# The end of a streaming encoder layer: the sample's stores on GpSimd's queue, the root as TensorE's diagonal, and the first piece of the last token block in halves

## The chip, the cores and the metric

The kernel runs on one core of one Trainium2 chip. The metric is the device time of one execution in microseconds (us). Three timed runs of the kernel before gave a median of 1300.93 us, the lowest 1300.31 and the highest 1302.64.

## The reference

One layer (DEPTH is 1) of a hybrid encoder runs on two request groups that share their weights: 256 new prompt positions (`x_prompt`) and 32 positions of a running stream (`x_sample`). Cut to what matters here:

```
D_MODEL = 2048;  SEQ = 256;  DEC_SEQ = 32;  D_FF = 5632;  EPS = 1e-6

def rmsnorm(x, g):
    y = xf * lax.rsqrt(jnp.mean(xf * xf, axis=-1, keepdims=True) + EPS)
    return (y * g).astype(x.dtype)

def run_layer(x, ...):
    xn = rmsnorm(x, norm_mix_pre);  proj = xn @ w_in
    y_pool = pool_mixer(...);  y_ssd = ssd_mixer(...)
    mix = concat[y_pool, y_ssd] @ w_out
    x = x + rmsnorm(mix, norm_mix_post)
    hn = rmsnorm(x, norm_ffn_pre)
    up = causal_dwconv(hn @ w_up, ...)
    f = (silu(gate) * val) @ w_down
    x = x + rmsnorm(f, norm_ffn_post)      # the part that the change touches
    return x, ...
```

The outputs are the two new `x` (`y_prompt` and `y_sample`, 32-bit floats) and the states of the pooling, the convolutions and the state-space mixer. The change touches only the last line: every row of `f` (one row per token, 2048 columns) has its sum of squares, the root of the mean, its reciprocal (the factor), the weights `norm_ffn_post`, and the residual `x`.

## The kernel before, in words

Everything up to the last product is held with features on the 128 partitions and the 288 tokens (256 of the prompt, 32 of the sample) along the free axis, 16 blocks of 128 features. The three large stages (`w_in`, `w_up`, `w_down`, and `w_out` between) stream their weights from memory through SP's queue in pieces of up to 1 MB; ScalarE and VectorE split each piece into a high and a low part (lines 153 and 154), and TensorE multiplies three times per block (line 167).

The end begins with the last two feature blocks of the down projection, A and B (lines 1300 to 1379). By then the other 14 blocks have been multiplied by their weights, turned through DRAM (`fd`) and loaded back with tokens on the partitions: `ft[2*q+b]` holds quarter `q` (512 columns) of token block `b` (128 tokens: `b` = 0 the first, `b` = 1 the last half of the prompt), `ft_s` the 32 sample tokens with their four quarters on four groups of 32 partitions. `xr[2*q+b]` and `xr_s` hold the residual in the same form, loaded long before.

For the last token block (`b` = 1) and the sample, A and B are computed first, their sums of squares go through TensorE (`other_sums`, line 1267), and `rf` (line 1276 the root on ScalarE, line 1277 the reciprocal on VectorE) is their factor. TensorE then goes on with the first token block (`b` = 0), whose 256 columns it computes with tokens on the partitions at once (`p_0`, line 1365). While it does, VectorE finishes the others: `y_out(q, b, rf)` writes `ft * rf + xr` into `xr` with one scalar_tensor_tensor of 128x512 (line 1385) and stores it on SP's queue (line 1386). The order before is quarters 0, 1 and 2 of `b` = 1, then the sample (line 1390, four stores at line 1392), then quarter 3.

When `p_0` is done, ScalarE squares it with a sum (line 1399), VectorE weighs it with `g_row` into `ft[6]` (line 1400), ScalarE takes the root and VectorE the reciprocal (lines 1276 and 1277 again, the factor of `b` = 0). Quarter 0 of `b` = 0 is TensorE's: `p_y` gets identity times `xr[0]` (line 1403) and, once ScalarE has scaled the identity by the factor (`diag`, line 1406), diag times `ft[0]` (line 1407). ScalarE copies `p_y` to SBUF (line 1408) and issues its store on its own queue (line 1411). Quarters 1, 2 and 3 of `b` = 0 are VectorE's, with `y_out`.

All of this is written between `pin(...)`, which keeps an engine's pinned instructions in the order of the program; SP's queue issues in that order too, and a store that waits holds up those behind it. Each token block has four quarters of 256 KB, the sample 256 KB in four stores of 64 KB.

Of the kernel before, what the change touches and what calls it, by code (L numbers as in the profile page):

```python
# [8 lines left out]
F32 = mybir.dt.float32  # L9
F32R = mybir.dt.float32r  # L10
AF = mybir.ActivationFunctionType
ALU = mybir.AluOpType
# [3 lines left out]
P = 128  # L16
TC = {"schedule_with_timeline_sim": True}
D_MODEL = 2048
# [52 lines left out]
def body(  # L71
# [23 lines left out]
    act, dve, pool, pe, sp = nc.scalar, nc.vector, nc.gpsimd, nc.tensor, nc.sync  # L95
# [36 lines left out]
    pin = tc.keep_in_program_order  # L132
# [90 lines left out]
    start = ExitStack()  # L223
# [41 lines left out]
    for name, n in COLS:  # L265
        c0 = sum(m.shape[1] for m in col.values())
# [9 lines left out]
    ident = const.tile([P, P], F32, name="ident")  # L276
# [3 lines left out]
        out=tri, in_=ones, pattern=[[1, P]], compare_op=ALU.is_ge, fill=0.0, base=0, channel_multiplier=-1  # L280
# [79 lines left out]
    for i, (kb, n) in enumerate(CHUNKS):  # L360
# [26 lines left out]
        for q, (r, m, k, x) in enumerate(products):  # L387
            if i == len(CHUNKS) - 1 and q == 0:
# [10 lines left out]
                start=kb + k + r + x == 0, stop=kb + k == KD - 1 and r == 1,  # L399
            ))  # L400

    for k in range(KD):
        c = slice(HEADS * (k % 4), HEADS * (k % 4 + 1))
# [7 lines left out]
    c0 = 3 * NXC + 3 * KD  # L411
# [82 lines left out]
    with tc.high_priority(offset=EVAC):  # L494
        for i, v in enumerate(v4):
            c = slice(HEADS * i, HEADS * (i + 1))
# [488 lines left out]
    for gi in range(2):  # L985
        c = slice(gi * P, (gi + 1) * P)
# [168 lines left out]
    fp = ffn.enter_context(tc.tile_pool(name="ffn", bufs=1))  # L1155
# [83 lines left out]
    xr = []  # L1239
# [8 lines left out]
    ft = [apool.tile([P, 512], F32, tag="a", name="ft") for _ in range(6)]  # L1248
# [25 lines left out]
    def factors(src, bias, n, name):  # L1274
        o = side1.tile([P, 2], F32, tag="trs", bufs=2, name=name)[:, :n]
        pin(act.activation(o, src, AF.Sqrt, bias=bias, scale=1.0 / D_MODEL))
        pin(dve.reciprocal(o, o))
        return o
# [40 lines left out]
    g_row = late_[:, 4 * P :]  # L1319
# [4 lines left out]
    p_0 = acc_ps.tile([P, 2 * P], F32, tag="acc", name="acc_t")  # L1324
# [12 lines left out]
    for n_, part_ in enumerate(parts):  # L1337
        for i, t in enumerate((A, B)):
            for k, hi, lo in part_:
                c, end = slice(i * P, (i + 1) * P), k == HALF - 1  # L1340
# [8 lines left out]
    bias_0 = fp.tile([P, 1], F32, name="bias_0")  # L1349
# [13 lines left out]
    for k, hi, lo in sum(parts, []):  # L1363
# [4 lines left out]
        if k == SUMS_AT:  # L1368
            other_sums(sq[0])
            rf = factors(p_f, eps_t, 2, "rf1")  # L1370
# [7 lines left out]
                    p_0[:, i * P : (i + 1) * P], part[t][:, C0], ident, start=False, stop=False, skip_group_check=True  # L1378
                ))

    def y_out(q, b, rf):

        x = xr[2 * q + b]
        f_ = last if (q, b) == (3, 1) else ft[2 * q + b]
        pin(dve.scalar_tensor_tensor(x, f_, rf, x, op0=ALU.mult, op1=ALU.add))  # L1385
        pin(sp.dma_start(out=y_prompt[0][b * P : (b + 1) * P, 512 * q : 512 * (q + 1)], in_=x))

    for q in range(3):
        y_out(q, 1, rf[:, 0:1])
    pin(dve.scalar_tensor_tensor(xr_s, ft_s, rf[:, 1:2], xr_s, op0=ALU.mult, op1=ALU.add))  # L1390
    for q in range(4):
        pin(sp.dma_start(
            out=y_sample[0][:, 512 * q : 512 * (q + 1)], in_=xr_s[NS * q : NS * (q + 1), :]
        ))
    y_out(3, 1, rf[:, 0:1])

    sum_0 = fp.tile([P, 1], F32, name="sum_0")
    sq_0 = fp.tile([P, 290], F32, tag="fc", bufs=6, name="sq_0")
    pin(act.activation(sq_0[:, : 2 * P], p_0, AF.Square, accum_out=sum_0))
    pin(dve.tensor_tensor(ft[6][:, 2 * P :], p_0, g_row, op=ALU.mult))  # L1400

    p_y = acc_ps.tile([P, 512], F32, tag="acc", name="py_")
    pin(pe.matmul(p_y, ident, xr[0], start=True, stop=False))
    rf = factors(sum_0, bias_0, 1, "rf0")
    diag = fp.tile([P, P], F32, tag="fc", bufs=6, name="diag")
    pin(act.activation(diag, ident, AF.Copy, scale=rf[:, 0:1]))
    pin(pe.matmul(p_y, diag, ft[0], start=False, stop=True))
    pin(act.activation(xr[0], p_y, AF.Copy))
    y_out(1, 0, rf[:, 0:1])
    y_out(2, 0, rf[:, 0:1])  # L1410
    pin(act.dma_start(out=y_prompt[0][0:P, 0:512], in_=xr[0]))
    y_out(3, 0, rf[:, 0:1])
    ffn.close()


# [65 lines left out]
```

## Time and profile before

| what | value |
|---|---|
| timed runs, median (lowest to highest) | 1300.93 us (1300.31 to 1302.64) |
| the profiled execution's own time | 1302.5 us |
| its span, first to last instruction | 1300.8 us |
| TensorE busy | 1292.3 us, 99% of the span |
| VectorE busy | 900.2 us, 69% |
| ScalarE busy | 670.9 us, 52% |
| GpSimd busy | 255.0 us, 20% |
| bytes over the DMA queues | 251.81 MB, mean 194 GB/s |
| granted TensorE clock | 1.000 |

Times in the trace count from the span's start. An instruction's row has its start, its duration, engine, line and operands; a row with "x3" merges three in a row. The "q" behind an engine (SPq, ACTq) marks its queue issuing a transfer: such a row says how long the issue took, not when the bytes arrived. That is in the groups of DMA issues, as microseconds from issue to landing. The view by windows gives the busy time of each engine and what the DMA engines moved in each stretch. The end that the change touches is the stretch from 1290 us on.

### The profile page before, as it was taken

The numbers are of one execution on the slowest core, as the hardware profiler recorded it, in microseconds if no ns is written. First come the engines' busy times: TensorE is split into PE (matmuls) and PEld (weight loads), VectorE is DVE, ScalarE is ACT, GpSimd is POOL, SyncE is SP. The second block draws the span as 40 slices with busy tenths as digits, with TensorE's granted clock in tenths as the row PEclk, the third lists the DMA queues.
The fourth block names the chain that finished last, engine by engine and source line by source line (L and its number), as shares of the span: only waits on it lengthen the run. The fifth ranks groups of instructions, "written<-read, shape, count | busy, mean of one in ns | idle before, by whom it ended". The sixth has DMA issues, their size and how long they took to land.

```text
span 1300.8 us, 25801 instructions
## 1 busy us (share of the span) xinstructions
PE 1292.3 (99%) x10283; PEld 1284.9 (99%) x10283; DVE 900.2 (69%) x1546; ACT 670.9 (52%) x1013; POOL 255.0 (20%) x407
## 2 busy tenths in 40 slices
PE   9999999999999999999999999999999999999998
PEld 9999999999999999999999999999999999999997
DVE  7899998998655688877766744336666666755454
ACT  7554976656544466544444443334444454444442
POOL 3433332122232231211211200001111121201110
PEclk9999999999999999999999999999999999999999
DMA  9578887355766478766545444555545555466763
GB/s 353 172 214 245 272 258 241 131 183 162 257 206 225 143 198 256 209 177 200 176 162 175 165 161 173 166 170 185 168 162 167 176 173 167 162 232 189 215 180 116
DMA packets 110648, 251.81 MB, mean 194 GB/s; under 512 B 65088, under 2 KB 74208, under 8 KB 88256
## 3 DMA queue, kind: packets, MB, share of 16 engines
q1 hardware_dynamic: 104144, 233.52, 55.9%
q0 software_dynamic: 5952, 16.13, 4.4%
q8 instruction: 80, 1.31, 0.4%
q10 hardware_dynamic: 432, 0.52, 0.1%
q14 instruction: 40, 0.33, 0.1%
HBM read 237.13 MB, written 13.00 MB: 192 GB/s over the span
## 4 chain that ended last, share of the span: by engine, by line
PE 95%; issue 2%; DMA 1%; ACT 1%; POOL 0%; DVE 0%; SPq 0%; POOLq 0%; ACTq 0%
PE acc L167 89%; PE acc L397 1%; DMA raw<-in_w_first 1%; PE acc_x L167 1%; PE acc_x L397 1%; PE acc L1342 1%; PE acc L1343 0%; DMA mg<-in_x_g 0%; PE py L678 0%; PE py_l L678 0%; PE acc_t L1365 0%; ACT w L330 0%; POOL ho L1073 0%; PE acc L404 0%; DVE xr L1385 0%
## 5 line engine op out<-in xcount | busy, mean ns | idle before, releaser
L154 DVE TENSOR_TENSOR wlo<-raw,whi 128x1024 fp32r<-128x1024 f32 (+1 forms) x396 | 472.7, 1196 | 285.6 <-ACT whi L153 284.7
L153 ACT ACTIVATE whi<-raw 128x1024 fp32r<-128x1024 f32 (+1 forms) x396 | 407.7, 1032 | 445.4 <-PE acc L167 362.6
L167 PE MATMUL acc<-hn,whi 128*128 128x288 f32 x2752 | 539.1, 294 | 0.7 <-ACT hn L1118 0.4
L167 PEld LDWEIGHTS acc<-hn,whi 128*128 128x128 f32 x2752 | 436.5, 188 | 1.8 <-ACT hn L1118 0.9
L167 PE MATMUL acc<-hn,wlo 128*128 128x288 f32 x1376 | 399.7, 291 | 0.0
L167 PEld LDWEIGHTS acc<-hn,wlo 128*128 128x128 f32 x1376 | 258.9, 188 | 0.0
L167 PE MATMUL acc<-fa,whi 128*128 128x288 f32 x1320 | 257.5, 293 | 0.0
L167 PE MATMUL acc<-xn,whi 128*128 128x288 f32 x1216 | 238.6, 294 | 0.0
L167 PEld LDWEIGHTS acc<-fa,whi 128*128 128x128 f32 x1320 | 208.9, 188 | 0.0
L167 PEld LDWEIGHTS acc<-xn,whi 128*128 128x128 f32 x1216 | 193.0, 188 | 0.6 <-issue 0.5
L167 PE MATMUL acc<-fa,wlo 128*128 128x288 f32 x660 | 192.1, 291 | 0.0
L167 PE MATMUL acc<-xn,wlo 128*128 128x288 f32 x608 | 177.4, 292 | 0.0
L167 PEld LDWEIGHTS acc<-fa,wlo 128*128 128x128 f32 x660 | 124.3, 188 | 0.0
L1168 POOL COPY fc_stage<-ebuf 128x4 f32<-128x4 f32 x88 | 26.3, 299 | 469.8 <-DVE ebuf L1167 448.2
L167 PEld LDWEIGHTS acc<-xn,wlo 128*128 128x128 f32 x608 | 114.5, 188 | 0.0
L167 PE MATMUL acc<-mixs,whi 128*128 128x288 f32 x512 | 100.2, 293 | 0.0
L1172 ACT ACTIVATE fc<-ebuf,cols 128x290 f32<-128x290 f32 x88 | 54.5, 623 | 78.2 <-DVE ebuf L1167 78.0
L1163 POOL COPY ebuf<-cols 128x2 f32<-128x2 f32 x88 | 71.7, 815 | 114.8 <-DVE fc L1174 98.8
L1174 DVE SCALAR_TENSOR_TENSOR fc<-ebuf,cols,fc 128x290 f32<-128x290 f32 x176 | 90.2, 516 | 4.2 <-ACT fc L1172 1.5
L167 PEld LDWEIGHTS acc<-mixs,whi 128*128 128x128 f32 x512 | 81.1, 188 | 0.0
L167 PE MATMUL acc<-mixs,wlo 128*128 128x288 f32 x256 | 74.6, 291 | 0.0
L167 PE MATMUL acc<-mixp,whi 128*128 128x288 f32 x256 | 50.1, 293 | 0.0
(313 smaller groups left out, 1250.9 us busy)
## 6 DMA issues: line engine op xcount, KB each, us to landing
raw<-in_w_up SPq DMA_DIRECT2D x80, 1024.0 KB, 5.2
raw<-in_w_in SPq DMA_DIRECT2D x38, 1024.0 KB, 5.4
raw<-in_w_down SPq DMA_DIRECT2D x32, 1024.0 KB, 4.9
raw<-in_w_out SPq DMA_DIRECT2D x22, 1024.0 KB, 5.2
raw<-in_w_down SPq DMA_DIRECT2D x16, 768.0 KB, 4.4
raw<-in_w_up SPq DMA_DIRECT2D x14, 512.0 KB, 4.5
gb<-g_d POOLq DMA_DIRECT2D x8, 832.0 KB, 8.0
raw<-in_w_first SPq DMA_DIRECT2D x5, 768.0 KB, 13.2
```

Source lines behind the costliest of these rows:

```text
L153: act.activation(hi, raw[:, k : k + n, :], AF.Copy)
L154: dve.tensor_tensor(lo, raw[:, k : k + n, :], hi.bitcast(F32), op=ALU.subtract)
L167: ins = pe.matmul(out, w, a[:, x, :], start=start and n == 0, stop=stop and n == 2)
L397: pin(pe.matmul(first[m], w[r][:, k, m * P : (m + 1) * P], xn[kb + k][:, x, :], start=kb + k + r + x == 0, stop=kb + k == KD - 1 and r == 1,))
L1163: pool.tensor_copy(e[:, 258:260], hist_f[:, :, i])
L1168: pool.tensor_copy(fc_stage[:, :, :, i], e[:, 256:324].rearrange("p (s c) -> p s c", c=34)[:, :, 0:2])
L1172: act.activation(c, e[:, 0:290], AF.Identity, bias=col["f_b"][:, i : i + 1], scale=f_w[:, 0, i : i + 1])
L1174: dve.scalar_tensor_tensor(c, e[:, r_ : r_ + 290], f_w[:, r_, i : i + 1], c, op0=ALU.mult, op1=ALU.add)
L1342: pin(pe.matmul(both, hi[:, c], f2[k][:, :, C1], start=k == 0, stop=end, skip_group_check=True))
```

## The change

Six edits, all behind the last large product:

- the four stores of the sample are issued by GpSimd's queue and not by SP's;
- VectorE computes the sample third, ahead of quarter 2 of the last token block, and no longer fourth;
- TensorE's piece (quarter 0 of the first token block) is computed as factor * (ft + root * xr): the identity multiplies `ft[0]`, the diagonal holds the root, and the factor is applied where ScalarE copies `p_y` out. The diagonal then waits for the root and not for its reciprocal;
- the diagonal's product and ScalarE's copy are done in two halves of 256 columns;
- quarter 1 of the first token block is computed and stored in two halves;
- the weighing of `p_0` is in two halves, the second one behind the two halves of quarter 1. The store of TensorE's piece stands in the program ahead of quarter 2.

```diff
-    def y_out(q, b, rf):
-        x = xr[2 * q + b]
+    def y_out(q, b, rf, pieces=1):
         f_ = last if (q, b) == (3, 1) else ft[2 * q + b]
-        pin(dve.scalar_tensor_tensor(x, f_, rf, x, op0=ALU.mult, op1=ALU.add))
-        pin(sp.dma_start(out=y_prompt[0][b * P : (b + 1) * P, 512 * q : 512 * (q + 1)], in_=x))
-    for q in range(3):
+        n = 512 // pieces
+        for c0 in range(0, 512, n):
+            c = slice(c0, c0 + n)
+            x = xr[2 * q + b][:, c]
+            pin(dve.scalar_tensor_tensor(x, f_[:, c], rf, x, op0=ALU.mult, op1=ALU.add))
+            pin(sp.dma_start(out=y_prompt[0][b * P : (b + 1) * P, 512 * q + c0 : 512 * q + c0 + n], in_=x))
+    for q in range(2):
         y_out(q, 1, rf[:, 0:1])
     pin(dve.scalar_tensor_tensor(xr_s, ft_s, rf[:, 1:2], xr_s, op0=ALU.mult, op1=ALU.add))
     for q in range(4):
-        pin(sp.dma_start(
+        pin(pool.dma_start(
             out=y_sample[0][:, 512 * q : 512 * (q + 1)], in_=xr_s[NS * q : NS * (q + 1), :]
         ))
-    y_out(3, 1, rf[:, 0:1])
+    for q in range(2, 4):
+        y_out(q, 1, rf[:, 0:1])
...
-    pin(dve.tensor_tensor(ft[6][:, 2 * P :], p_0, g_row, op=ALU.mult))
+    halves = (slice(0, P), slice(P, 2 * P))
+    def weigh(c):
+        pin(dve.tensor_tensor(ft[6][:, 2 * P + c.start : 2 * P + c.stop], p_0[:, c], g_row[:, c], op=ALU.mult))
+    weigh(halves[0])
     p_y = acc_ps.tile([P, 512], F32, tag="acc", name="py_")
-    pin(pe.matmul(p_y, ident, xr[0], start=True, stop=False))
-    rf = factors(sum_0, bias_0, 1, "rf0")
+    pin(pe.matmul(p_y, ident, ft[0], start=True, stop=False, skip_group_check=True))
+    root = fp.tile([P, 1], F32, name="root_0")
+    rf = fp.tile([P, 1], F32, name="rf_0")
+    pin(act.activation(root, sum_0, AF.Sqrt, bias=bias_0, scale=1.0 / D_MODEL))
+    pin(dve.reciprocal(rf, root))
     diag = fp.tile([P, P], F32, tag="fc", bufs=6, name="diag")
-    pin(act.activation(diag, ident, AF.Copy, scale=rf[:, 0:1]))
-    pin(pe.matmul(p_y, diag, ft[0], start=False, stop=True))
-    pin(act.activation(xr[0], p_y, AF.Copy))
-    y_out(1, 0, rf[:, 0:1])
-    y_out(2, 0, rf[:, 0:1])
+    pin(act.activation(diag, ident, AF.Copy, scale=root))
+    for c in (slice(0, 2 * P), slice(2 * P, 4 * P)):
+        pin(pe.matmul(p_y[:, c], diag, xr[0][:, c], start=False, stop=True, skip_group_check=True))
+    for c in (slice(0, 2 * P), slice(2 * P, 4 * P)):
+        pin(act.activation(xr[0][:, c], p_y[:, c], AF.Copy, scale=rf))
+    y_out(1, 0, rf, 2)
+    weigh(halves[1])
     pin(act.dma_start(out=y_prompt[0][0:P, 0:512], in_=xr[0]))
-    y_out(3, 0, rf[:, 0:1])
+    y_out(2, 0, rf)
+    y_out(3, 0, rf)
```

Three places show how it moves the instructions. The first is the end of SP's queue, whose last loads are those of `ft` and `ft_s`; "out<-xr" are stores of the prompt, "out<-xr_s" those of the sample.

```order
 L1262 DMA ft_15303<-fd 128x256
 L1263 DMA ft_s<-fd 32x256
-L1386 DMA out<-xr 128x512 x3
-L1392 DMA out<-xr_s 32x512 x4
-L1386 DMA out<-xr 128x512 x4
-L1469 UNCONDITIONAL_BRANCH
+L1389 DMA out<-xr 128x512 x4
+L1389 DMA out<-xr 128x256 x2
+L1389 DMA out<-xr 128x512 x2
```

The sample's four stores have left SP's queue: quarter 3 of the last token block is no longer behind them, and the piece that was one store of 128x512 is two of 128x256. On GpSimd they stand behind its last sums of the squares, and only the first of them waits for VectorE:

```order
 L774 TENSOR_TENSOR fsum<-fsum,sq 128x288 [waits Activation_49]
 L774 TENSOR_TENSOR fsum<-fsum,sq 128x288 [waits Activation_49,Pool_49] x12
-L1469 UNCONDITIONAL_BRANCH
-L1469 ISA [waits barrier_Pool_Activation_PE_DVE_SP_gather]
+L1395 DMA out<-xr_s 32x512 [waits DMAHW2_49,DMASW4_49,DVE_49]
+L1395 DMA out<-xr_s 32x512 [waits DMAHW4_49,DMASW5_49]
+L1395 DMA out<-xr_s 32x512 [waits DMAHW5_49,DMASW6_49]
+L1395 DMA out<-xr_s 32x512 [waits DMAHW6_49,DMASW7_49]
```

The DMA semaphores named there are the counters of earlier transfers. Third, VectorE from the sample on, in the kernel before (`pft` is quarter 3 of the last token block, `late` is `ft[6]`, `acc_t` is `p_0`):

```order
L1385 SCALAR_TENSOR_TENSOR xr<-ft,rf_15459,xr 128x512 [waits DMAHW2_49]
L1390 SCALAR_TENSOR_TENSOR xr_s<-ft_s,rf_15459,xr_s 128x512 [waits DMAHW7_49,DMAHW3_49,Activation_49]
L1385 SCALAR_TENSOR_TENSOR xr<-pft,rf_15459,xr 128x512 [waits PE_49]
L1400 TENSOR_TENSOR late<-acc_t,late 128x256 [waits DMAHW4_49,Activation_49]
L1277 RECIPROCAL rf_15508<-rf_15508 128x1 [waits Activation_49]
L1385 SCALAR_TENSOR_TENSOR xr<-ft,rf_15508,xr 128x512 [waits DVE_49]
L1385 SCALAR_TENSOR_TENSOR xr<-ft,rf_15508,xr 128x512 [waits DMAHW1_49]
L1385 SCALAR_TENSOR_TENSOR xr<-late,rf_15508,xr 128x512 [waits DMAHW5_49]
```

and in the changed kernel:

```order
L1393 SCALAR_TENSOR_TENSOR xr_s<-ft_s,rf_15459,xr_s 128x512 [waits DMAHW7_49,DMAHW3_49,Activation_49]
L1388 SCALAR_TENSOR_TENSOR xr<-ft,rf_15459,xr 128x512 [waits DMAHW2_49]
L1388 SCALAR_TENSOR_TENSOR xr<-pft,rf_15459,xr 128x512 [waits PE_49]
L1407 TENSOR_TENSOR late<-acc_t,late 128x128 [waits DMAHW4_49,Activation_49]
L1415 RECIPROCAL rf_15509<-root_15508 128x1 [waits Activation_49]
L1388 SCALAR_TENSOR_TENSOR xr<-ft,rf_15509,xr 128x256 [waits DVE_49]
L1388 SCALAR_TENSOR_TENSOR xr<-ft,rf_15509,xr 128x256
L1407 TENSOR_TENSOR late<-acc_t,late 128x128
L1388 SCALAR_TENSOR_TENSOR xr<-ft,rf_15509,xr 128x512 [waits DMAHW1_49]
L1388 SCALAR_TENSOR_TENSOR xr<-late,rf_15509,xr 128x512 [waits DMAHW5_49,DVE_49]
```

The sample has moved one place up; between the reciprocal and the last two quarters stand two half pieces and half of the weighing, where one whole piece stood. On the other engines the order differs in the rows of the diff alone.

## The prediction

> **What bounds the kernel now.** I began with the page's span and its chain of waits: TensorE carries nearly all of it, and the end is a short tail behind it.
>
> ```profile
> span 1300.8 us, 25801 instructions
> PE 95%; issue 2%; DMA 1%; ACT 1%; POOL 0%; DVE 0%; SPq 0%; POOLq 0%; ACTq 0%
> ```
>
> The change leaves every large product alone, so the question is what ends last in the tail. Second, the timeline from 1291 us on (start, duration, engine):
>
> ```profile
> 1292.03 0.75 DVE L1390 SCALAR_TENSOR_TENSOR xr_s<-ft_s,rf,xr_s 128x512 f32<-128x512 f32 x1
> 1292.69 0.74 DVE L1385 SCALAR_TENSOR_TENSOR xr<-pft,rf,xr 128x512 f32<-128x512 f32 x1
> 1293.46 0.42 DVE L1400 TENSOR_TENSOR late<-acc_t,late 128x256 f32<-128x256 f32 x1
> 1293.80 0.15 DVE L1277 RECIPROCAL rf<-rf 128x1 f32<-128x1 f32 x1
> 1293.99 1.42 DVE L1385 SCALAR_TENSOR_TENSOR xr<-ft,rf,xr 128x512 f32<-128x512 f32 x2
> 1295.32 0.75 DVE L1385 SCALAR_TENSOR_TENSOR xr<-late,rf,xr 128x512 f32<-128x512 f32 x1
> 1290.82 1.66 SPq L1386 DMA_DIRECT2D out<-xr  x3
> 1292.81 1.75 SPq L1392 DMA_DIRECT2D out<-xr_s  x4
> 1294.66 1.86 SPq L1386 DMA_DIRECT2D out<-xr  x4
> 1296.23 0.35 ACTq L1411 DMA_DIRECT2D out<-xr  x1
> ```
>
> The engines are done at 1296.2 us; only stores follow. SP is the late one: VectorE ends quarter 3 of the last block at 1292.69 + 0.74 = 1293.43, but SP, busy with the sample's four issues, issues its store at 1294.66, 1.23 us later. Third, the windows of half a microsecond (the last figure of a row is the GB/s moved):
>
> ```profile
> 1291.50:1292.00 0.50, 0.50 (x7) 0.50 (x6) 0.50 (x1) 0.00 (x0) 0.00 (x0) 1.00 0.67 250
> ...
> 1294.00:1294.50 0.50, 0.06 (x1) 0.06 (x1) 0.50 (x1) 0.39 (x1) 0.00 (x0) 1.00 0.58 135
> 1294.50:1295.00 0.50, 0.50 (x2) 0.24 (x2) 0.50 (x2) 0.00 (x0) 0.00 (x0) 1.00 0.55 131
> 1295.00:1295.50 0.50, 0.50 (x2) 0.00 (x0) 0.50 (x2) 0.00 (x0) 0.00 (x0) 1.00 0.53 131
> 1295.50:1296.00 0.50, 0.07 (x1) 0.00 (x0) 0.50 (x1) 0.39 (x1) 0.00 (x0) 1.00 0.93 340
> 1296.00:1296.50 0.50, 0.00 (x0) 0.00 (x0) 0.07 (x1) 0.20 (x1) 0.00 (x0) 1.00 1.05 385
> 1296.50:1297.00 0.50, 0.00 (x0) 0.00 (x0) 0.00 (x0) 0.00 (x0) 0.00 (x0) 1.00 1.03 377
> 1297.00:1297.50 0.50, 0.00 (x0) 0.00 (x0) 0.00 (x0) 0.00 (x0) 0.00 (x0) 1.00 1.00 381
> 1297.50:1298.00 0.50, 0.00 (x0) 0.00 (x0) 0.00 (x0) 0.00 (x0) 0.00 (x0) 1.00 1.02 377
> 1298.00:1298.50 0.50, 0.00 (x0) 0.00 (x0) 0.00 (x0) 0.00 (x0) 0.00 (x0) 1.00 1.06 393
> 1298.50:1299.00 0.50, 0.00 (x0) 0.00 (x0) 0.00 (x0) 0.00 (x0) 0.00 (x0) 1.00 0.98 352
> 1299.00:1299.50 0.50, 0.00 (x0) 0.00 (x0) 0.00 (x0) 0.00 (x0) 0.00 (x0) 1.00 0.05 16
> ```
>
> From 1294.0 to 1295.5 the transfers run at a third of their rate, since only the sample's small stores are in flight; from 1295.5 on they run full. The eight rows from 1295.50 add to 0.5 us x 2621 GB/s = 1.31 MB, which is five pieces of 256 KB: quarter 3 of the last block and the whole first block. So **the tail is bound by a backlog of stores**: 1.31 MB at about 380 GB/s, 0.69 us a piece, 3.45 us, begun late. Fourth, the landings:
>
> ```profile
> out<-xr SPq DMA_DIRECT2D x1, 256.0 KB, 2.1
> out<-xr SPq DMA_DIRECT2D x1, 256.0 KB, 3.2
> out<-xr ACTq DMA_DIRECT2D x1, 256.0 KB, 3.3
> ```
>
> The first is the store of 1290.82 alone, the others the last two. The last lands at 1296.23 + 3.3 = 1299.53 and the span ends 1.27 us later. Its data ends near 1299.02 (8 KB in the last window), so 0.5 us lie between last byte and landing. The first data comes at about 1291.67 (125 KB in the row of 1291.50, 0.33 us at 381 GB/s), 0.85 us after the issue of 1290.82.
>
> **The change part by part.** *Sample third, on GpSimd's queue.* SP loses four issues, 1.75 us, at the place where quarter 3 waited for them. VectorE's five pieces of the last block and the sample keep their sum; pieces stand 0.66 us apart (1292.03 to 1292.69). The sample is ready 0.66 us earlier, at 1292.12; quarter 2 at 1292.78, and its store goes from about 1292.14 to 1292.81; quarter 3 stays at 1293.43 and its store goes from 1294.66 to 1293.47, **1.2 us earlier**. On GpSimd the issue of a store from SBUF to memory has no row; the nearest are loads from that queue, and its accumulating loads beside VectorE:
>
> ```profile
> L1022 POOL DMA_DIRECT2D xq<-xs_d x24: 496/498/537, 315.0 to 439.7; - x24
> DMA to landing us min/median/max: 2.7/4.2/7.9
> 480.28 2.67 DVE L1137 TENSOR_TENSOR mg<-mg,rm 128x288 f32<-128x288 f32 x7
> 481.02 1.76 POOL L1141 DMA_DIRECT2D mg<-in_x_g  x2 [3.17 <-DVE mg L1137]
> 482.12 4.25 POOL L1141 DMA_DIRECT2D mg<-in_x_g  x4
> out<-xr_s SPq DMA_DIRECT2D x4, 64.0 KB, 1.7
> ```
>
> L1022 has the sample's 32 partitions, in pieces of 32 KB: 0.5 us an issue, 2.7 to 7.9 us to landing, the 7.9 in a stage full of weights. I take 0.5 us and 2.7 us, the row where little else is in flight: issues at 1292.15, 1292.65, 1293.15 and 1293.65, the last landing at 1296.35, hidden under the prompt's stores. Without that cover it would end the kernel; the upper bound is 1293.65 + 7.9 = 1301.55, 2.0 us after today's last landing. Nothing is queued behind these four on GpSimd, and its last sums are long done.
>
> A page speaks against this part. By the Trainium skill, "DMA: Bandwidth & Descriptors", section "SWDGE vs HWDGE vs iDMA", GpSimd writes the descriptors of its transfers into SBUF, and VectorE can lock it out there in its two-port modes; "SBUF — State Buffer", section "Who interferes with whom", adds that two SBUF inputs contend only with GpSimd's reads. The trace agrees with the second sentence: VectorE runs two-input operations without a gap from 480.28 to 482.95, and GpSimd issues at 481.02 and, two issues on, at 482.12, 0.55 us each. All of VectorE's pieces in the tail have two tensor inputs, so by row and page alike the stores aren't locked out. Were they, the third rival gives the price.
>
> *The root as diagonal, in halves.*
>
> ```profile
> 1292.95 0.38 ACT L1399 ACTIVATE sq<-acc_t 128x256 f32<-128x256 f32 x1 [1.95 <-PE acc_t L1365]
> 1293.46 0.29 ACT L1276 ACTIVATE rf<-sum,bias 128x1 f32<-128x1 f32 x1
> 1293.99 0.40 ACT L1406 ACTIVATE diag<-ident,rf 128x128 f32<-128x128 f32 x1 [0.23 <-DVE rf L1277]
> 1294.44 1.13 PE L1407 MATMUL py__15506<-ft,diag 128*128 128x512 f32 x2 [0.67 <-ACT diag L1406]
> 1295.61 0.60 ACT L1408 ACTIVATE xr<-py__15506 128x512 f32<-128x512 f32 x1 [1.22 <-PE py__15506 L1407]
> ```
>
> The root ends at 1293.75; the diagonal starts at about 1293.79 instead of 1293.99 (0.20 us less, the hop over VectorE). TensorE's product ends 0.2 us earlier, plus some 0.1 us for the second weight load: 1295.47. The copy of the second half then costs 0.38 us (L1399 reads 128x256 of PSUM in that) where the whole cost 0.60. The store goes from 1296.23 to about **1295.87, 0.35 us earlier**. Bounds: nothing, if the per-partition factor makes the copy or the extra loads slower by what is saved; 0.5 us, if the loads are hidden. The first half's copy lies beside the second half's product.
>
> *Quarter 1 in halves, the weighing in halves.* An instruction of 512 columns takes 0.745 us and one of 256 takes 0.42; back to back each loses 0.085 us, so two halves cost 0.67 us against 0.66, and two weighings of 128 columns (0.26 us each by the same slope) 0.35 against 0.34. But the second weighing now stands behind the reciprocal, where the wait for the root hid it before: the last two quarters come **0.18 us later**, at 1295.59 and 1296.25 (up to 0.35 us if the halves gain no overlap). Halves of quarter 1 are issued at 1294.43 and 1294.78, where its whole store waited for SP until 1295.13.
>
> **The sum.** With first data 0.85 us after issue and 0.69 us a piece, the data runs: quarters 0 and 1 of the last block 1291.67 to 1293.02, quarters 2 and 3 from 1293.66 and 1294.32 to 1295.01, the halves from 1295.28 and 1295.63 to 1295.98. The sample's 0.69 us fits into the gaps (0.64 us before 1293.66, 0.27 us before 1295.28, 0.49 us after 1295.98). The last three pieces are issued at 1295.62, 1295.87 and 1296.28; their data starts at 1296.47 and takes 2.07 us: 1298.54, landing at 1299.04. Before: 1299.53. **The change gains about 0.5 us.** The profiled execution took 1302.5 us, 1.7 more than its span; it lies 1.57 us above the median of the runs, 1300.93, so I set the difference against both: 1302.0 for an execution like the profiled one, **1300.5 us** for the median. The runs shown spread by 2.33 us (1300.31 to 1302.64), so a change of under 0.2% (2.6 us) can't be told from none, and this one is a fifth of that.
>
> **The rivals.**
>
> *The stream ends where it did.* Nine pieces of 256 KB at 0.69 us must leave after 1291.67: 6.2 us, 1297.9 without a gap. If GpSimd's small stores come to the transfer engines only after 1296.47 they push the last three pieces by up to 0.69 us, and the gain of 0.5 us becomes a loss of 0.2: 1300.9 to 1301.1. For it speaks the 1.0 us by which the landings of L1022 lie above the 1.7 us of SP's stores of 64 KB; against it, that the first issue is 4.3 us ahead of that point.
>
> *A larger gain.* If the prompt's stores run ahead of the sample's and leave no backlog, only the last issue counts: 1296.28 + 2.1 = 1298.4, 1.1 us less than before: 1299.8. Against it: three pieces in 0.66 us of issues need 2.07 us of data.
>
> *GpSimd's stores land last (slower).* If its issue is held while VectorE works, to 1296.25, four issues and a landing give 1296.25 + 2.0 + 2.7 = 1300.95, 1.4 us later than today: 1302.3; with the landing of 7.9 us and no hold, 2.0 us: 1302.9. It decides from the point where the last of the four lands after 1299.5, 5.9 us after its issue. For it: L1022's maximum; against it: the row of L1141, and that the tail moves no weights.
>
> *The change doesn't reach the end*, because another wait (SP's four last issues, 0.49 us apart in 1.86 us) takes the place: the last SP issue depends on VectorE at 1296.25, not on SP, which is free from 1295.2; 1300.9.
>
> **How the numbers follow.** Gain of about 0.5 us: 0.55 (its own range 1299.6 to 1301.4 with the spread of the runs); no gain, by the stream or by another wait: 0.22; larger gain: 0.08; GpSimd last: 0.12; something outside the tail, of either sign, since the instructions ahead of it keep their order but the placement of two new small tiles may not leave everything as it was: 0.03. Only the last and the far end of GpSimd's case, with the spread on top, pass 0.2%: faster 0.04, within 0.2% 0.91, slower 0.05. The range takes in most of GpSimd's case and the spread below: 1299.2 to 1302.0.
>
> **What would show it.** SP's store of quarter 3 of the last block near 1293.5 on this clock, and the windows from 1294.0 to 1295.5 well above 135 GB/s. GpSimd's issues 0.5 us apart, in the stretch where VectorE works; the last landing of the sample before the prompt's. The diagonal straight behind the root, the copy's second half ending near 1295.85, the last VectorE piece near 1296.25. Last landing about 0.5 us earlier, and the 1.27 us behind it unchanged. I am wrong if a store of the sample lands last, if the span after the last landing grows, or if time moves ahead of 1290 us.

## The result

| kernel | median us | lowest to highest | runs |
|---|---|---|---|
| before | 1301.47 | 1300.31 to 1302.64 | 22 |
| changed | 1303.81 | 1302.38 to 1305.12 | 22 |

The changed kernel takes 1.0017 times the time before, 95% interval 1.0011 to 1.0023: about 2.3 us slower (1.4 to 3.0 us). That is under the 0.2% that the prediction called no difference, but it is clear of noise, it has the other sign, and it lies outside the range of 1299.2 to 1302.0.

The tail of the changed kernel, by the timeline, as for before:

```profile
1289.38 0.75 DVE L1393 SCALAR_TENSOR_TENSOR xr_s<-ft_s,rf,xr_s 128x512 f32<-128x512 f32 x1
1290.42 2.05 POOL L1395 DMA_DIRECT2D out<-xr_s  x4 [15.29 <-DVE xr_s L1393]
1290.96 0.38 ACT L1403 ACTIVATE sq<-acc_t 128x256 f32<-128x256 f32 x1 [1.96 <-PE acc_t L1365]
1291.80 0.40 ACT L1417 ACTIVATE diag<-ident,root 128x128 f32<-128x128 f32 x1
1292.25 1.13 PE L1419 MATMUL py__15506<-xr,diag 128*128 128x256 f32 x4 [0.47 <-ACT diag L1417]
1293.42 0.84 ACT L1421 ACTIVATE xr<-py__15506,rf 128x256 f32<-128x256 f32 x2 [1.22 <-PE py__15506 L1419]
1293.65 0.74 DVE L1388 SCALAR_TENSOR_TENSOR xr<-late,rf,xr 128x512 f32<-128x512 f32 x1
1294.29 0.35 ACTq L1424 DMA_DIRECT2D out<-xr  x1
1294.59 0.39 SPq L1389 DMA_DIRECT2D out<-xr  x1
```

Absolute times of two profiled executions can't be laid side by side: here the square of `p_0` starts at 1290.96, in the kernel before at 1292.95, while everything that leads to it stands in the same order. I therefore count from that square, the last thing that the change leaves alone, and call the stretch to the end of the span the **tail**: 1300.8 - 1292.95 = 7.85 us before, 1301.2 - 1290.96 = 10.24 us now. The difference, 2.39 us, is that of the medians (2.34 us) to within 0.05 us, so the loss is in the tail.

And the stores don't end last. The last one is issued at 1294.59 and the group of DMA issues for it reads

```profile
out<-xr SPq DMA_DIRECT2D x1, 256.0 KB, 3.8
```

It lands at 1298.4, and the span ends at 1301.2: 2.8 us lie behind the last landing, where 1.27 us lay before. What fills them is in a view that the prediction never opened, the closing instructions of the program, which have the line of the kernel's call. First the changed kernel (count, shortest/median/longest in ns, first and last start):

```profile
L1483 POOLq DRAIN  x1: 8447/8447/8447, 1291.9 to 1291.9; - x1
L1483 SPq DRAIN  x3: 7/7/7, 1298.9 to 1300.6; - x3
L1483 POOLq EVENT_SEMAPHORE  x4: 17/17/17, 1300.4 to 1301.1; - x4
L1483 ACTq EVENT_SEMAPHORE  x2: 17/17/17, 1300.6 to 1301.1; - x2
```

then the kernel before:

```profile
L1469 POOLq DRAIN  x1: 8789/8789/8789, 1275.9 to 1275.9; - x1
L1469 SPq DRAIN  x3: 7/7/7, 1299.9 to 1300.3; - x3
L1469 POOLq EVENT_SEMAPHORE  x4: 17/17/17, 1300.0 to 1300.7; - x4
L1469 ACTq EVENT_SEMAPHORE  x2: 17/17/17, 1300.2 to 1300.7; - x2
```

Each engine closes with a DRAIN and then meets the others at a barrier of semaphores. On SP a DRAIN takes 7 ns. On GpSimd the first one takes 8.4 to 8.8 us. Before, it began with GpSimd's last sum at 1275.9 and was over at 1284.7, 15 us ahead of the barrier. In the changed kernel GpSimd's last instruction is the sample's fourth store, the DRAIN begins beside it at 1291.9 and ends at 1300.35; SP has been ready since 1298.9, and the barrier opens at 1300.4. From there to the end of the span it is 0.8 us in both.

The view of SP's waits puts its last 1.7 us down to TensorE's queue (first row below; total us, times, longest us). But a wait that covers several engines is put down to one of them, and the first closing DRAINs of the three others were over by 1294.9, which leaves GpSimd:

```profile
SPq L1483 <- PEq L1483: 2.1, 2, 1.7
L1483 PEldq DRAIN  x1: 1175/1175/1175, 1292.3 to 1292.3; - x1
L1483 DVEq DRAIN  x1: 1324/1324/1324, 1293.1 to 1293.1; - x1
L1483 ACTq DRAIN  x1: 153/153/153, 1294.7 to 1294.7; - x1
```

### The profile page after: what moved, and what is told of

The parts are those of the page before. It is cut to its first block, busy times and chain, and to the rows that moved or that the text cites. A ratio compares the mean times of both kernels' runs of the same rounds, so it can differ in the third digit from the quotient of the medians.

```text
span 1301.2 us, 25815 instructions
## 1 busy us (share of the span) xinstructions
PE 1290.9 (99%) x10285; PEld 1284.3 (99%) x10285; DVE 900.5 (69%) x1548; ACT 671.2 (52%) x1014; POOL 258.5 (20%) x411
## 4 chain that ended last, share of the span: by engine, by line
PE 97%; DMA 1%; ACT 1%; DVE 0%; issue 0%; SPq 0%; DVEq 0%; ACTq 0%
PE acc L167 91%; PE acc L397 1%; PE acc_x L167 1%; DMA raw<-in_w_first 1%; PE acc_x L397 1%; PE acc L1342 1%; PE acc L1343 0%; PE py L678 0%; PE acc_t L1365 0%; PE py_l L678 0%; ACT w L330 0%; PE pst L1054 0%; PE acc L404 0%; DVE rm L1105 0%; DVE w L334 0%; PE py_s L697 0%
```

## The experiments

The theory after the result, called "drain" in the expectations: GpSimd's closing DRAIN runs 7.6 to 7.9 us past its last instruction, and ends last when that instruction comes late. The rivals were that only transfers of GpSimd's queue have to be waited out, that the change's other edits or the addresses of its new tiles cost the time, or that any late instruction on GpSimd does. Eight kernels were run, four at a time beside the kernel before, whose median was 1301.44 us in the first four and 1301.26 us in the others.

**The sample back on SP's queue.** The changed kernel with one edit undone:

```diff
-        pin(pool.dma_start(
+        pin(sp.dma_start(
             out=y_sample[0][:, 512 * q : 512 * (q + 1)], in_=xr_s[NS * q : NS * (q + 1), :]
```

> The changed kernel with one edit undone: the sample's four stores go back to SP's queue, everything else of the change stays. Tail = from the start of ScalarE's square of p_0 to the end of the span: 7.85 us before, 10.24 us in the changed kernel. Theory 'drain' (GpSimd's closing DRAIN runs about 7.6 to 7.9 us past GpSimd's last instruction and now ends last): the tail falls to 7.3 to 8.0 us and the time is 0.5 us under to 0.2 us over the kernel before. Rival 'other edits' (the halves, the root as diagonal or the placement of the new tiles cost the 2.3 us): the time stays about 2.3 us above before and the tail near 10 us.

Measured: 1300.98 us, ratio 0.9996 (0.9987 to 1.0006); the tail is 1298.8 - 1291.10 = 7.70 us. The queue of the sample's stores is the whole loss. It also shows what the other five edits are worth together: 0.15 us of tail, in one execution of each kernel, and nothing that the times can tell. Its timeline:

```profile
1291.10 0.38 ACT L1403 ACTIVATE sq<-acc_t 128x256 f32<-128x256 f32 x1 [1.95 <-PE acc_t L1365]
1293.55 0.84 ACT L1421 ACTIVATE xr<-py__15506,rf 128x256 f32<-128x256 f32 x2 [1.22 <-PE py__15506 L1419]
1294.42 0.35 ACTq L1424 DMA_DIRECT2D out<-xr  x1
1294.59 0.40 SPq L1389 DMA_DIRECT2D out<-xr  x1
```

The group of DMA issues for the store of 1294.59, and GpSimd's closing instruction, which is again 24 us ahead of the barrier:

```profile
out<-xr SPq DMA_DIRECT2D x1, 256.0 KB, 3.2
```

```profile
L1483 POOLq DRAIN  x1: 8802/8802/8802, 1274.1 to 1274.1; - x1
```

ScalarE issues the store of TensorE's piece 3.32 us after the square; before it was 1296.23 - 1292.95 = 3.28. So the root as diagonal and the halves gained nothing either, which the fifth point below takes up. The last landing is at 1294.59 + 3.2, 6.7 us after the square, against 6.6 before; 1.0 us lie behind it, where it was 1.27.

**The sample's stores on GpSimd's queue alone.** The same line the other way round, in the kernel before (the sample stays fourth on VectorE):

```diff
-        pin(sp.dma_start(
+        pin(pool.dma_start(
             out=y_sample[0][:, 512 * q : 512 * (q + 1)], in_=xr_s[NS * q : NS * (q + 1), :]
```

> The kernel before with one edit of the change alone: the sample's four stores on GpSimd's queue, the sample still fourth. Theory 'drain': its last issue ends near 1294.9 on the clock of the profile before, 0.7 us later relative to p_0 than in the changed kernel, so the tail is about 10.8 us and the time 2.7 to 3.1 us above before. Rival 'software queue', by the landing of the last store (up to 3.9 us after its issue): the tail follows the last landing, near 8 us. Rival 'other edits': the time is that of before.

Measured: 1304.36 us, ratio 1.0023 (1.0014 to 1.0033), 2.9 us above before; the tail is 1303.1 - 1292.21 = 10.89 us. Its square and its DRAIN:

```profile
1292.21 0.38 ACT L1399 ACTIVATE sq<-acc_t 128x256 f32<-128x256 f32 x1 [1.95 <-PE acc_t L1365]
L1469 POOLq DRAIN  x1: 8447/8447/8447, 1293.8 to 1293.8; - x1
```

The DRAIN starts 1.6 us after the square, where it was 1.0 in the changed kernel, and the tail is 0.65 us longer: about the 0.66 us by which the sample comes later on VectorE. The edit alone makes the loss, and the tail follows GpSimd's last instruction.

**A copy of 8 bytes a partition on GpSimd, no transfer.** Added to the kernel before, at three places:

```diff
+    gp_out = side1.tile([P, 2], F32, name="gp_out")
+    pin(pool.tensor_copy(gp_out, xr_s[:, 0:2]))
     y_out(3, 1, rf[:, 0:1])
```

> The kernel before plus one tiny copy on GpSimd (128x2) that reads the sample's result; nothing else, no transfer moved. Theory 'drain': the copy starts near 1292.8 on the clock of the profile before and ends 0.3 to 0.8 us later; its closing DRAIN ends 7.6 to 7.9 us after that, near 1301 us, and the span 0.8 us later: 0.9 to 1.5 us slower than before. Rival 'software queue' (only transfers issued by GpSimd have to be waited out at the end): no change, within 0.2 us in the tail.

The late copy is the same two lines, behind the last `y_out` and reading `xr[6]`:

> As the copy in the middle, but the tiny GpSimd copy reads VectorE's very last piece, near 1296.1 on the clock of the profile before. Theory 'drain': 1296.1 + 0.3 to 0.8 + 7.6 to 7.9 + 0.8 us, so a tail of 11.9 to 12.7 us and 4.0 to 4.8 us slower than before. Rival 'software queue': no change.

Measured: 1321.11 us (ratio 1.0148, 1.0133 to 1.0163) and 1324.41 us (1.0173, 1.0158 to 1.0189), 20 and 23 us slower, which neither theory had. The tails say something else: 1319.4 - 1310.91 = 8.5 us and 1322.9 - 1311.12 = 11.8 us, both a little under the theory's (8.7 to 9.4 us, by the first expectation, and 11.9 to 12.7), since the copy takes only 0.19 us. The other 18 to 19 us had gone by when the square began. What these two had that the change hasn't is a new tile in a pool (`side1`) that is opened early, so that the addresses of the tiles that are placed behind it can move. So the copies were run again with the tile in the pool opened last:

```diff
-    gp_out = side1.tile([P, 2], F32, name="gp_out")
+    gp_out = fp.tile([P, 2], F32, name="gp_out")
```

> As the tiny GpSimd copy of the sample's result added to the kernel before, but its 8-byte tile lies in the pool that is opened last, so that no other tile's address moves. Theory 'drain' with the length that the first copy showed (its DRAIN lasts 7.8 us from the copy's start, the span ends 0.8 us later): tail from the square of p_0 to the end of the span 8.4 to 8.5 us against 7.85 before, and 0.4 to 0.9 us slower than before. Rival 'the copy itself or its place in the stream costs the 19.7 us of the first copy': about 20 us slower again. If instead the 17 us ahead of the tail came from the tile's address, they are gone here.

> The same tiny copy, reading the factor of the last token block, 2.9 us ahead of the square of p_0. Theory 'drain': its DRAIN ends 2.9 us less than 7.8 us after the square, at 4.9 us, before the last store lands at 6.6 us: hidden, tail 7.8 to 7.9 us, time within 0.3 us of before. Rival 'any GpSimd instruction in the tail costs': slower by as much as the copy in the middle.

This early copy reads `rf` and stands ahead of the last block's first quarter.

> The same tiny copy, reading VectorE's last piece, 3.15 us behind the square of p_0. Theory 'drain': 3.15 + 7.8 + 0.8 us, a tail of 11.7 to 11.8 us, 3.7 to 4.3 us slower than before; the difference to the copy in the middle is the 3.3 us by which it starts later. Rival 'a fixed cost per kernel with a late GpSimd instruction': as the copy in the middle.

| copy of GpSimd | its start, us after the square | tail us | expected tail | time us | ratio (95%) |
|---|---|---|---|---|---|
| none (before) | | 7.85 | | 1301.26 | |
| early | -2.9 | 7.80 | 7.8 to 7.9 | 1301.57 | 1.0003 (0.9994 to 1.0012) |
| middle | -0.1 | 8.46 | 8.4 to 8.5 | 1301.74 | 1.0003 (0.9994 to 1.0012) |
| late | 3.2 | 11.81 | 11.7 to 11.8 | 1306.41 | 1.0038 (1.0024 to 1.0051) |

The rows behind the table, early first, then middle and late: from the timeline the copy and the square, from the closing instructions the DRAIN.

```profile
1290.21 0.19 POOL L1389 COPY gp_out<-rf 128x2 f32<-128x2 f32 x1 [12.95 <-DVE rf L1277]
1293.10 0.38 ACT L1401 ACTIVATE sq<-acc_t 128x256 f32<-128x256 f32 x1 [1.95 <-PE acc_t L1365]
```

```profile
L1471 POOLq DRAIN  x1: 7811/7811/7811, 1290.2 to 1290.2; - x1
```

```profile
1291.52 0.19 POOL L1396 COPY gp_out<-xr_s 128x2 f32<-128x2 f32 x1 [15.72 <-DVE xr_s L1390]
1291.64 0.38 ACT L1401 ACTIVATE sq<-acc_t 128x256 f32<-128x256 f32 x1 [1.95 <-PE acc_t L1365]
```

```profile
L1471 POOLq DRAIN  x1: 7811/7811/7811, 1291.5 to 1291.5; - x1
```

```profile
1295.37 0.18 POOL L1414 COPY gp_out<-xr 128x2 f32<-128x2 f32 x1 [19.01 <-DVE xr L1385]
1292.19 0.38 ACT L1399 ACTIVATE sq<-acc_t 128x256 f32<-128x256 f32 x1 [1.95 <-PE acc_t L1365]
```

```profile
L1471 POOLq DRAIN  x1: 7809/7809/7809, 1295.3 to 1295.3; - x1
```

A copy of 0.19 us that nothing waits for makes the kernel 0.4% slower when it comes last, and costs nothing when it comes 6 us sooner. The DRAIN has the same 7.81 us each time, and no transfer is needed for it: the rival "software queue" falls, and so does "any late instruction costs". From the middle to the late copy the start moves by 3.3 us and the tail by 3.35 us. The times move more: by 4.7 us, and the late copy is 5.2 us above before where 3.7 to 4.3 were expected. The intervals of the ratios hold both figures, and why five timed runs of the late copy lie higher isn't shown. The 20 us of the first pair came with the tile's place, since with the tile elsewhere they are gone.

**The stores on ScalarE's and SP's queues.** The changed kernel with two edits: no transfer on GpSimd, and TensorE's piece in two PSUM tiles:

```diff
-        pin(pool.dma_start(
+        pin((act if q < 2 else sp).dma_start(
...
-    p_y = acc_ps.tile([P, 512], F32, tag="acc", name="py_")
-    pin(pe.matmul(p_y, ident, ft[0], start=True, stop=False, skip_group_check=True))
+    p_ys = [acc_ps.tile([P, 2 * P], F32, tag="acc", name="py_") for _ in range(2)]
+    for i in range(2):
+        pin(pe.matmul(p_ys[i], ident, ft[0][:, 2 * P * i : 2 * P * (i + 1)], start=True, stop=False, skip_group_check=True))
...
+        pin(pe.matmul(p_ys[i], diag, xr[0][:, c], start=False, stop=True, skip_group_check=True))
...
+        pin(act.activation(xr[0][:, c], p_ys[i], AF.Copy, scale=rf))
```

> The changed kernel with two edits: the sample's stores are issued two by ScalarE's queue and two by SP's (none by GpSimd), and TensorE's piece lies in two PSUM tiles of 256 columns, so that the first half's copy can start while TensorE does the second. Theory: no late GpSimd instruction, so the end is the last store's landing again. ScalarE's first copy starts at about 1.9 us after the square of p_0 (2.46 in the changed kernel) and the store of TensorE's piece is issued at 2.9 (3.33); SP's store of quarter 3 of the last block at about 0.5; the last three pieces' data start at 3.7 and take 2.07 us: last landing at 6.2 to 6.4 us against 6.6 before, tail 7.4 to 7.6 us, time 0.2 to 0.5 us under before. Rival 'the stores are bound by their bytes whatever the order': landing at 6.6 us and the time of before.

Its timeline:

```profile
1291.96 0.85 ACTq L1395 DMA_DIRECT2D out<-xr_s  x2
1292.86 0.38 ACT L1403 ACTIVATE sq<-acc_t 128x256 f32<-128x256 f32 x1 [2.05 <-PE acc_t L1365]
1294.14 0.70 PE L1420 MATMUL py__15506<-xr,diag 128*128 128x256 f32 x2 [0.55 <-ACT diag L1418]
1294.68 0.59 PE L1420 MATMUL py__15507<-xr,diag 128*128 128x256 f32 x2
1294.88 0.47 ACT L1422 ACTIVATE xr<-py__15506,rf 128x256 f32<-128x256 f32 x1 [0.79 <-PE py__15506 L1420]
1295.31 0.47 ACT L1422 ACTIVATE xr<-py__15507,rf 128x256 f32<-128x256 f32 x1
1295.82 0.36 ACTq L1425 DMA_DIRECT2D out<-xr  x1
1296.32 0.33 SPq L1389 DMA_DIRECT2D out<-xr  x1
```

and the DMA issue of the last of them:

```profile
out<-xr SPq DMA_DIRECT2D x1, 256.0 KB, 2.7
```

The first copy starts 2.02 us after the square, beside the second half's product, and the store is issued at 2.96. The last store lands at 1296.32 + 2.7, 6.2 us after the square, and the tail is 1300.1 - 1292.86 = 7.24 us, 0.6 us shorter than before and a little under the 7.4 to 7.6 that were expected. About 0.1 us of this is not a gain: ScalarE is busy with its two issues until 1292.81, so the square itself starts late, 0.35 us after VectorE's piece of quarter 3 (1292.51), where it was 0.26 before. The 0.5 us that are left are the size of the gain that the prediction had worked out, with the sample's stores on other queues and with two tiles. The time is 1300.80 us, ratio 0.9996 (0.9987 to 1.0005): what the trace shows is too small for the times to prove, and this version isn't shown to beat the kernel before.

## Why the prediction was wrong

**The step that failed is "Nothing is queued behind these four on GpSimd".** Behind them stood GpSimd's own end of the program. The sum asked when the last store lands and took the 1.27 us behind it as fixed; it measured 2.8, the sign of being wrong that the prediction itself had named. In the changed kernel's times the end is 1291.9 + 8.45 for the DRAIN + 0.8 for the barrier = 1301.15, and the span ends at 1301.2. The row was in the profile of before, with its 8.8 us, among instructions that the page does not count as busy. An estimate from it was within reach: the DRAIN runs 8.79 - 1.16 = 7.6 us past the end of GpSimd's last sum, the forecast's last issue ends at 1293.65 + 0.5 = 1294.15, and with the 0.8 us the span ends at 1302.6, 1.8 us later than before and not 0.5 us sooner. The measured 2.4 us are more because GpSimd's first issue starts 0.29 us after the sample's piece is done (1290.13 to 1290.42, where the forecast had 0.03) and because the DRAIN runs 7.9 us past an issue.

**The sign of the "GpSimd last" rival was right, its mechanism wrong.** It had GpSimd's stores land last. They land 2.6 to 3.9 us after their issue (2.7, the lowest of the load row, was taken; its median was 4.2), the last at about 1295.9, 2.5 us ahead of the prompt's last. It priced the case at 1.4 to 2.0 us; the measured 2.3 us is near that by accident.

**No lock-out: right.** GpSimd issues four stores in 2.05 us while VectorE works through two-input operations, 0.5 us each, as the load rows of before had it. The Trainium skill, "SBUF — State Buffer", section "Who interferes with whom", says of VectorE's operations with two SBUF inputs that they contend only with GpSimd instructions that read SBUF; the trace agrees, as far as it shows no issue held up.

**The stream was mis-sized.** The prediction let the sample's bytes fill gaps at the rate of all others. The queues' share of the transfer engines in the changed kernel, 1291.5 to 1294.5 us (packets, MB, share of 16 engines):

```profile
q1 hardware_dynamic: 270, 0.49, 45.2%
q0 software_dynamic: 105, 0.23, 40.9%
```

GpSimd's queue takes nearly as much of the engines for 0.23 MB as SP's for 0.49: 1.9 times the engine time for a byte. SP's five stores from 1291.47 on land 3.7 to 4.2 us after their issue, not 2.1 to 3.2, and the last landing comes 7.4 us after the square, 0.8 us later than before, where 0.5 us sooner was forecast. Of that miss of 1.3 us, 0.3 are the last issue (3.63 us after the square, forecast 3.33), the rest is the slower landing. With the stores on other queues (the first and the last experiment) the last landing is at 6.7 and 6.2. The rival "the stream ends where it did" had the kind of this, pieces pushed back by GpSimd's, and priced it at 0.2 us. By the last landing alone the change would have lost without the DRAIN too; that is an estimate, no run has it. Why the packets take longer isn't shown here.

**TensorE's halves: the overlap was assumed.** Forecast: the store of TensorE's piece 0.35 us sooner. Measured: 1294.29 - 1290.96 = 3.33 us after the square, against 3.28. The diagonal did follow the root at once, and its product started 0.2 us sooner (1.29 us after the square against 1.49), but the first copy starts at 1293.42, when both halves are done at 1293.38, and two copies take 0.84 us where one took 0.60. The order of the changed kernel had told it: of the two copies only the first waits for TensorE.

```
L1421 ACTIVATE xr<-py__15506,rf_15509 128x256 [waits DVE_49,PE_49]
L1421 ACTIVATE xr<-py__15506,rf_15509 128x256
```

One wait that covers both copies has to be for both products. In the last experiment, with a tile for each half, each copy has its own, and the first starts 0.04 us after the first half's product ends (1294.84 to 1294.88).

**VectorE's halves: right in kind, under-sized.** The last quarter starts 2.69 us after the square (1293.65), before 2.37 (1295.32): 0.32 us later, where 0.18 was taken and 0.35 was the bound. **SP's queue: right.** Freed of the sample it issues quarter 3 of the last block 0.51 us after the square, where the forecast had 0.52.

## What to carry to other kernels

Ask of the last instruction on every engine, not only of the last store, what the engine still has to do behind it: in this kernel GpSimd needs some 8 us to close, and work on it is free up to about 9 us ahead of the end and costs its full delay after that. Read the closing instructions of the profile before an engine that had been idle is given the last job. And a piece cut in halves overlaps only if the waits are cut too, which the order shows beforehand.

## What the runs showed of the hardware that was not expected

GpSimd's first closing DRAIN, which starts beside its last instruction, takes 7.81 us with a copy of 0.19 us, 8.79 with a sum of 1.16 us, and 8.45 with a store's issue of 0.50 us: it ends 7.6 us past the end of a compute instruction and 7.9 us past the end of an issue. In the kernel before, VectorE's longest is 2.1 us, and SP's are 7 ns.

A tile of 8 bytes a partition in an early pool made the part ahead of the tail 18 to 19 us longer, although the order of the work on VectorE, ScalarE and SP was the same as before. It is spread over the products. Here is one group of them in the kernel before, then with the copy in the middle and its tile in the early pool, then with the tile in the pool opened last:

```profile
L167 PE MATMUL acc<-hn,whi 128*128 128x288 f32 x2752 | 539.1, 294 | 0.7 <-ACT hn L1118 0.4 <-ACT whi L153 0.2
```

```profile
L167 PE MATMUL acc<-hn,whi 128*128 128x288 f32 x2752 | 547.5, 296 | 0.7 <-ACT hn L1118 0.4 <-ACT whi L153 0.2
```

```profile
L167 PE MATMUL acc<-hn,whi 128*128 128x288 f32 x2752 | 538.7, 294 | 0.6 <-ACT hn L1118 0.4
```

In the second its idle time is the same as in the first, its busy time 8.4 us longer. Which tiles moved, and why a product then takes longer, was not tried.
